# Eighteen block pairs in the MLP, with the copies, additions and gate parts around them placed anew

## The chip, the cores and the metric

One core of a Trainium2 chip runs the kernel. The metric is the device time of one execution in microseconds; several executions are taken, and their median is compared. The core has five engines that run side by side, each in the order of its own instruction list: PE (matmuls), DVE, ACT, POOL and SP. SP only issues transfers here; ACT and POOL can issue some too. Engines wait for each other through semaphores.

## The reference, cut to what matters

One layer of a decoder over 512 positions with model width 1024: a token-mixing half (sparse attention and a gated short convolution, merged by gates and projected by `w_o`), a layer norm, and then the half that the change is about:

```python
h = layer_norm(DEEPNORM_ALPHA * h + merged @ w_o[i], ln1_g[i], ln1_b[i])
gu = causal_dwconv(h @ w_ffn_up[i], ffn_conv_w[i], ffn_conv_b[i])
g_ffn, u_ffn = jnp.split(gu, 2, axis=-1)
ffn = (jax.nn.silu(g_ffn) * u_ffn) @ w_ffn_down[i]
ple = jax.nn.sigmoid(h @ w_ple_gate[i] + b_ple_gate[i]) * (p[i] @ w_ple[i])
h = layer_norm(DEEPNORM_ALPHA * h + ffn + ple, ln2_g[i], ln2_b[i])
```

`w_ffn_up` is 1024 x 5632 (2816 gate columns and 2816 up columns), `w_ffn_down` 2816 x 1024. All is float32.

## The kernel before, in words

**Precision.** Each matrix is split into a high part and a remainder, both in the matmul's 32-bit format, and a product is three matmuls: high by high, high by low, low by high. For weights `Chunk` does this: SP loads a raw tile `wr` of 128 x 1024 (L54; four buffers), ACT casts it to `wh` (L74), and DVE or POOL subtracts to get `wl` (L141). There are four buffers of `wh` and `wl`; a chunk is split up to three steps ahead of its use, if a buffer is free.

**Steps.** The program is a list of steps, and each engine gets its instructions in this order. For step i: first the splits (and loads) that are due (`advance`), then the functions registered for the step in `preps`, then the step's own matmuls and what follows them. Steps 0 to 5 are index queries, 6 (`at_first`) to 43 attention queries, convolution, attention, gates and branches. Steps 44 (`at_wo`) to 47 are the first column half of `w_o` for all four blocks of 128 positions, 24 matmuls a step; behind step 47 DVE adds the residual and takes statistics (L924, L186). Steps 48 to 51 are the second half, one block of positions a step. Behind the matmuls of each, DVE adds and normalises that block (`ln1`, L947, L931, L932), and PE transposes the block before it (`ln1_T`, tile xT). Step 52 is `ple1`. Steps 53 (`at_ple`) to 64 are the gate `h @ w_ple_gate`, and from 65 (`at_ff`) the up-projection's 22 pairs of a gate column tile and an up column tile follow, then the down-projection.

**Products with one block fewer.** Where two column tiles and two halves of the positions make a 2 x 2 block product, seven products of sums replace eight (`by_blocks`). A plain pair j takes two steps of 24 matmuls with 512 columns each. A pair in `BY_BLOCKS` (2 to 18) takes three steps of 24 and one of 12 matmuls with 256 columns, and needs two chunks that are sums of blocks of the weights. These sums are made in DRAM ahead of time: SP copies blocks into `ws` (`weight_copy`, two transfers of 256 KB each), and POOL issues transfers that add to them (`weight_add`, four of 256 KB a pair). The gate (sums by `gate_sums` on DVE of tiles `pgr` that `gate_load` brings, four times 512 KB) and the down-projection (`sum_copy`, `sum_add`, 24 each, 512 KB, tiles `sd`) do the same. The pairs' sums are made in two groups, `pairs[0]` (the first `EARLY`) and `pairs[1]`.

**Order of transfers.** `at_step(at, f, eng)` puts a transfer into step `at`; with an engine it is tied to that engine's progress: the engine writes a token, POOL reads it (tile behind, L1319) and then issues. Before, the early copies stood in steps 6 to 20, the early additions in 21 to 40, the copies of the late pairs in 30 to 40, their additions every fourth step from 63, all 24 copies of `sd` from 55 to 72, and the first 12 additions of `sd` every sixth step from 69. `gate_load` stood in steps 42 and 43, `gate_sums` in 45 and 46. The three tiles `pw` were loaded back in step 52 (L966). The gate's end (`gate_mult`, L1039; `gate_add`, L1043; four parts) stood in steps 68 to 74.

Of the kernel before, what the change touches and what calls it, by code (L numbers as in the profile page):

```python
# [11 lines left out]
OP = mybir.AluOpType  # L12
# [71 lines left out]
class Kern:  # L84
# [409 lines left out]
    def plan(self):  # L494
        nc, a = self.nc, self.a
# [321 lines left out]
        early = [(wa(8 + i, lo="vp"[i], resident=True), kind) for i, kind in enumerate("cx")]  # L817
# [27 lines left out]
        at_first = len(self.steps)  # L845
# [116 lines left out]
        def ple1(pc, w):  # L962
            def f():
                self.pw = [[self.k4(f"pw{h}{i}", F32, (P, 2, 512)) for i in range(2)] for h in range(2)]
                for i in range(3):
                    nc.sync.dma_start(self.pw[i // 2][i % 2], self.pwdram[i].rearrange("p (b n) -> p b n", b=2))  # L966
                act = [[t.rearrange("p (k t) -> p k t", k=2)[:, k] for t in (pc.hi, pc.lo)] for k in range(2)]
                for b in range(2, NB):
                    tb = slice(b * P, (b + 1) * P)
                    o = self.ps("ple")  # L970
                    for k in range(2):
                        wh, wl = (t.rearrange("p (k n) -> p k n", k=2)[:, k] for t in (w.hi, w.lo))
                        self.mm3(o, act[k][0][:, tb], act[k][1][:, tb], wh, wl, k == 0, k == 1)
                    nc.scalar.copy(self.pw[1][b // 2][:, b % 2], o)
            return f
# [6 lines left out]
        def gate_load(u):  # L982
            def f():
                gate_raw[u] = [self.k4(f"pgr{u}{i}") for i in range(4)]
                for i, t in enumerate(gate_raw[u]):
                    nc.sync.dma_start(t, a["w_b"][10 + 2 * i + u])
            return f

        def gate_sums(u):

            def f():
                ra, rb, rc, rd = gate_raw[u]
                for to, x, y in ((rd, rc, rd), (rc, ra, rc), (ra, ra, rd), (rb, rb, ra)):
                    nc.vector.tensor_tensor(to, x, y, op=OP.add)
            return f

        for u in range(2):
            self.preps.setdefault(at_wo - 2 + u, []).append(gate_load(u))
            self.preps.setdefault(at_wo + 1 + u, []).append(gate_sums(u))
        self.hblock, self.hsum = {}, {}  # L1000
        first_gate = [wb(10 + u, resident="halves", lo="p", lead=9) for u in range(2)]
        pc, w = chunk(a["p_T"]), wb(9)
# [1 line left out]

        at_ple = len(self.steps)
        self.gsum, self.gacc = {}, {}
        GATE = {"a": ("X", 0, 0), "b": ("Y", 1, 0), "cd": ("Z", None, 0), "acd": ("X", None, 2),
                "abcd": ("Z", 1, 1), "ac": ("X", None, 1), "d": ("X", None, 3)}

# [31 lines left out]
        def gate_add(f, t, i):  # L1041
            h = self.h1[2 * t + i][:, f * 512:f * 512 + 512]
            nc.vector.scalar_tensor_tensor(h, h, ALPHA, self.gsum[f, t][:, i], op0=OP.mult, op1=OP.add)  # L1043
# [115 lines left out]

        BY_BLOCKS = list(range(2, 19))
        EARLY = 13
        wsum = {j: [self.dram.tile([P, 1024], F32, name=f"ws{i}{j}", tag=f"ws{i}{j}") for i in range(2)]
                for j in BY_BLOCKS}

# [95 lines left out]
        def sum_copy(n, i):  # L1262
            return lambda: nc.sync.dma_start(sd[n][i], wd[base[n], i])

        def sum_add(n, i):
            return lambda: nc.gpsimd.dma_start(sd[n][i], adds[n](i), accum_op=OP.add, max_dma_last_dim=4096)

        at_ff = len(self.steps)
        self.row_sums = row_sums
# [2 lines left out]
            self.preps.setdefault(at_ple + at, []).append(f)  # L1272

        parts_of = [(0, 0), (0, 1), (1, 1), (1, 0)]
        for f, at in ((gate_bias, (6, 10, 13, None)), (gate_sigmoid, (7, 11, 14, 15)), (gate_mult, (15, 16, 18, 20)),
                      (lambda f, t: gate_add(f, t, 0), (15, 17, 19, 21)), (lambda f, t: gate_add(f, t, 1), (16, 17, 19, 21))):
            for x, n in zip(parts_of, at):
                if n is not None:
                    self.preps.setdefault(at_ple + n, []).append(lambda f=f, x=x: f(*x))
# [42 lines left out]

        pairs = BY_BLOCKS[:EARLY], BY_BLOCKS[EARLY:]
        for n, (j, i) in enumerate((j, i) for i in range(2) for j in pairs[0]):
            at_step(at_first + 15 * n // (2 * EARLY), weight_copy(j, i))
        for n, (j, i) in enumerate((j, i) for i in (0, 1, 3, 2) for j in pairs[0]):
            at_step(at_first + 15 + 21 * n // 56, weight_add(j, i), nc.vector)
        for n, (j, i) in enumerate((j, i) for j in pairs[1] for i in range(2)):  # L1330
            at_step(at_first + 24 + n * 3 // 2, weight_copy(j, i))
        for n, (j, i) in enumerate((j, i) for j in pairs[1] for i in (0, 1, 3, 2)):
            at_step(at_ff - 2 + 4 * n, weight_add(j, i), nc.scalar)
        for n, (name, i) in enumerate(copies):
            at_step(at_ple + 2 + n * 3 // 4, sum_copy(name, i))
            at = (4 + 6 * n if n < 12 else n_ff - 6 + (n - 12) * 5 // 4 if n < 17 else n_ff + 1 + 3 * (n - 17))
            at_step(at_ff + at, sum_add(name, i), nc.scalar)


        TAILC = 4  # L1340
# [289 lines left out]
```

## Time and profile before

| | |
|---|---|
| Median of 3 runs | 749.59 us (749.45 to 753.15) |
| Profiled execution | 751.02 us, span 749.3 us |
| Granted clock of PE, mean | 0.994 of full speed |
| PE busy | 736.3 us (98%) |
| DVE, ACT, POOL busy | 606.6, 403.6, 233.5 us |
| DMA | 172.48 MB, 230 GB/s mean |

The span runs from the first to the last instruction; the execution's time is a little longer. Matmuls overlap, so a busy PE isn't one at its peak; the distance between the starts of matmuls is the better measure. Tiles are named without their numbers: `pgr` is any of the gate's raw tiles. "x4" is the number of instructions that a row merges, and in brackets stands how long the engine was idle before them and what ended that. SPq is SP's list of issues.

### The profile page before, as it was taken

The numbers are of one execution on the slowest core, as the hardware profiler recorded it, in microseconds if no ns is written. First come the engines' busy times: TensorE is split into PE (matmuls) and PEld (weight loads), VectorE is DVE, ScalarE is ACT, GpSimd is POOL, SyncE is SP. The second block draws the span as 40 slices with busy tenths as digits, with TensorE's granted clock in tenths as the row PEclk, the third lists the DMA queues.
The fourth block names the chain that finished last, engine by engine and source line by source line (L and its number), as shares of the span: only waits on it lengthen the run. The fifth ranks groups of instructions, "written<-read, shape, count | busy, mean of one in ns | idle before, by whom it ended". The sixth has DMA issues, their size and how long they took to land.

```text
span 749.3 us, 11574 instructions
## 1 busy us (share of the span) xinstructions
PE 736.3 (98%) x4159; PEld 640.4 (85%) x4159; DVE 606.6 (81%) x1031; ACT 403.6 (54%) x671; POOL 233.5 (31%) x294
## 2 busy tenths in 40 slices
PE   9999999999999999998999999999999999999995
PEld 5998888888888888887888899999999988888885
DVE  5877999865666366769997899999998888978797
ACT  4557334457566325233465567676676653655540
POOL 4314656542412545435300122333311112121002
PEclk9999999999999999999999999999999999999998
DMA  9372597679756989993576999888997877999661
GB/s 350 103 279 99 169 382 233 203 222 212 165 102 159 254 222 305 319 370 113 204 302 206 345 266 270 239 256 215 239 266 217 232 219 171 265 266 281 223 212 56
DMA packets 57257, 172.48 MB, mean 230 GB/s; under 512 B 6720, under 2 KB 6848, under 8 KB 56816
## 3 DMA queue, kind: packets, MB, share of 16 engines
q1 hardware_dynamic: 41664, 135.29, 50.8%
q0 software_dynamic: 14384, 34.22, 25.3%
q10 hardware_dynamic: 1152, 2.25, 0.8%
q8 instruction: 32, 0.52, 0.3%
q14 instruction: 25, 0.20, 0.1%
HBM read 165.95 MB, written 66.58 MB: 310 GB/s over the span
## 4 chain that ended last, share of the span: by engine, by line
PE 49%; DVE 2%; DMA 1%; issue 0%; POOL 0%; ACT 0%; DVEq 0%; ACTq 0%
PE ffb L1212 20%; PE dn L1385 5%; PE dn L1384 5%; PE dn L1386 5%; PE ff L155 2%; PE ff L156 2%; PE ff L157 2%; PE pg L1026 2%; PE pg L1024 2%; PE pg L1025 2%; DMA wr<-in_w_a 1%; PE xT L122 1%; PE wo L799 1%; PE wo L800 1%; PE wo L801 1%; DVE ff L708 0%
## 5 line engine op out<-in xcount | busy, mean ns | idle before, releaser
L74 ACT CAST wh<-wr 128x1024 fp32r<-128x1024 f32 (+1 forms) x179 | 176.3, 990 | 98.8 <-PE dn L1386 21.0
L141 DVE TENSOR_TENSOR wl<-wr,wh 128x1024 fp32r<-128x1024 f32 (+1 forms) x162 | 191.1, 1195 | 34.7 <-ACT wh L74 33.7
L1319 POOL TENSOR_TENSOR behind<-token,neghalf 128x1 f32<-128x1 f32 x92 | 51.4, 588 | 306.9 <-ACT token L1318 208.5
L1212 PE MATMUL ffb<-hsl,wh 128*128 128x256 f32 x272 | 77.0, 283 | 0.0
L1212 PE MATMUL ffb<-hsh,wh 128*128 128x256 f32 x272 | 77.0, 283 | 0.0
L1212 PE MATMUL ffb<-hsh,wl 128*128 128x256 f32 x272 | 77.0, 283 | 0.0
L1212 PE MATMUL ffb<-h1T,wh 128*128 128x256 f32 x408 | 75.2, 284 | 0.8 <-ACT c L1235 0.8
L1212 PEld LDWEIGHTS ffb<-h1T,wh 128*128 128x128 f32 x408 | 63.6, 192 | 1.5 <-ACT c L1235 1.4
L141 POOL TENSOR_TENSOR wl<-wr,wh 128x1024 fp32r<-128x1024 f32 (+1 forms) x21 | 49.2, 2353 | 35.9 <-ACT wh L74 35.9
L1212 PE MATMUL ffb<-h1T,wl 128*128 128x256 f32 x204 | 57.7, 283 | 0.0
L1212 PEld LDWEIGHTS ffb<-hsh,wh 128*128 128x128 f32 x272 | 52.2, 192 | 0.0
L1212 PEld LDWEIGHTS ffb<-hsl,wh 128*128 128x128 f32 x272 | 52.2, 192 | 0.0
L1212 PEld LDWEIGHTS ffb<-hsh,wl 128*128 128x128 f32 x272 | 52.2, 192 | 0.0
L155 PE MATMUL gt<-hT,wh 128*128 128x512 f32 x128 | 50.6, 395 | 0.1
L157 PE MATMUL gt<-hT,wl 128*128 128x512 f32 x128 | 49.9, 390 | 0.0
L156 PE MATMUL gt<-hT,wh 128*128 128x512 f32 x128 | 49.8, 389 | 0.0
L1212 PEld LDWEIGHTS ffb<-h1T,wl 128*128 128x128 f32 x204 | 39.1, 192 | 0.0
L173 POOL TENSOR_TENSOR rstd<-veps,neghalf 128x1 f32<-128x1 f32 x12 | 11.7, 979 | 81.6 <-DVE veps L171 42.8
L1185 POOL DMA_DIRECT2D ws<-in_w_a x34 | 32.0, 1189 | 3.4 <-issue 3.0
L1185 POOL DMA_DIRECT2D ws<-ws x34 | 31.1, 1072 | 2.3 <-DVE sig L785 0.9
L155 PE MATMUL cv<-hT,wh 128*128 128x512 f32 x80 | 31.4, 392 | 0.0
L155 PE MATMUL ff<-h1T,wh 128*128 128x512 f32 x80 | 31.1, 389 | 0.0
(337 smaller groups left out, 2021.0 us busy)
## 6 DMA issues: line engine op xcount, KB each, us to landing
wr<-in_w_a SPq DMA_DIRECT2D x63, 512.0 KB, 4.9
ws<-in_w_a SPq DMA_DIRECT2D x68, 256.0 KB, 6.4
wr<-ws SPq DMA_DIRECT2D x34, 512.0 KB, 6.2
ws<-in_w_a POOLq DMA_DIRECT2D x34, 256.0 KB, 8.2
ws<-ws POOLq DMA_DIRECT2D x34, 256.0 KB, 7.7
wr<-in_w_b SPq DMA_DIRECT2D x15, 512.0 KB, 11.4
wr<-in_w_dn SPq DMA_DIRECT2D x15, 512.0 KB, 5.6
wr<-in_w_a SPq DMA_DIRECT2D x17, 256.0 KB, 6.4
```

What stands on the lines that cost most here:

```text
L74: nc.scalar.copy(hi, raw)
L141: (self.nc.vector if eng == "v" else self.nc.gpsimd).tensor_tensor(lo, raw, hi.bitcast(F32), op=OP.subtract)
L155: t.matmul(out, wh, xh, start=start, stop=False)
L156: t.matmul(out, wh, xl, start=False, stop=False)
L157: t.matmul(out, wl, xh, start=False, stop=stop)
L1024: nc.tensor.matmul(o, xh, wh, start=first, stop=False, skip_group_check=True)
L1185: return lambda: nc.gpsimd.dma_start(to, what, accum_op=OP.add, max_dma_last_dim=4096)
L1212: nc.tensor.matmul(o, l[:, c], r, start=start and c + i == 0, stop=stop and c == 3 and i == 2, skip_group_check=True)
L1319: nc.gpsimd.tensor_tensor(self.sm("behind", [P, 1], bufs=2), t, self.neghalf, op=OP.mult)
L1384: nc.tensor.matmul(o, ah, wh[:, i, c], start=first, stop=False, skip_group_check=bank == "X")
L1385: nc.tensor.matmul(o, ah, wl[:, i, c], start=False, stop=False, skip_group_check=bank == "X")
L1386: nc.tensor.matmul(o, al, wh[:, i, c], start=False, stop=last, skip_group_check=bank == "X")
```

## The change

- `BY_BLOCKS` begins at pair 1 instead of 2, so there are 18 block pairs, and `EARLY` is 14 instead of 13; four late pairs remain.
- 28 early weight copies and, between them, the 12 `sd` copies `cd` and `abcd` are put into steps 3 to 19. The early additions (56 instead of 52) follow in steps 21 to 41.
- The copies of the late pairs move to steps 48 to 51. The other 12 `sd` copies stand in steps 54 to 65, one each.
- From step 63 on, additions follow about every 1.83 steps: one of a late pair and one half (512 columns) of `ac` or `acd` in turn; these 12 additions become 24 of 256 KB.
- `gate_load(0)` moves from step 42 to 41 (`gate_load(1)` stays in 43), `gate_sums` from 45 and 46 to 44 and 45.
- The loads of `pw` move from step 52 to 54, 55 and 56, one each.
- The gate's last parts spread: multiplications in steps 66, 70, 74 and 79 instead of 68, 69, 71 and 73, additions up to step 83 instead of 74. A block pair begins at step 69, so the parts fall into block pairs 1 to 4 and the steps before.

```diff
--- before.py
+++ after.py
@@ -962,8 +962,6 @@
         def ple1(pc, w):
             def f():
                 self.pw = [[self.k4(f"pw{h}{i}", F32, (P, 2, 512)) for i in range(2)] for h in range(2)]
-                for i in range(3):
-                    nc.sync.dma_start(self.pw[i // 2][i % 2], self.pwdram[i].rearrange("p (b n) -> p b n", b=2))
                 act = [[t.rearrange("p (k t) -> p k t", k=2)[:, k] for t in (pc.hi, pc.lo)] for k in range(2)]
                 for b in range(2, NB):
                     tb = slice(b * P, (b + 1) * P)
@@ -995,8 +993,8 @@
             return f
 
         for u in range(2):
-            self.preps.setdefault(at_wo - 2 + u, []).append(gate_load(u))
-            self.preps.setdefault(at_wo + 1 + u, []).append(gate_sums(u))
+            self.preps.setdefault(at_wo - 3 + 2 * u, []).append(gate_load(u))
+            self.preps.setdefault(at_wo + u, []).append(gate_sums(u))
         self.hblock, self.hsum = {}, {}
         first_gate = [wb(10 + u, resident="halves", lo="p", lead=9) for u in range(2)]
         pc, w = chunk(a["p_T"]), wb(9)
@@ -1004,6 +1002,12 @@
 
         at_ple = len(self.steps)
         self.gsum, self.gacc = {}, {}
+
+        def ple_back(i):
+            return lambda: nc.sync.dma_start(self.pw[i // 2][i % 2], self.pwdram[i].rearrange("p (b n) -> p b n", b=2))
+
+        for i in range(3):
+            self.preps.setdefault(at_ple + 1 + i, []).append(ple_back(i))
         GATE = {"a": ("X", 0, 0), "b": ("Y", 1, 0), "cd": ("Z", None, 0), "acd": ("X", None, 2),
                 "abcd": ("Z", 1, 1), "ac": ("X", None, 1), "d": ("X", None, 3)}
 
@@ -1159,8 +1163,8 @@
 
 
 
-        BY_BLOCKS = list(range(2, 19))
-        EARLY = 13
+        BY_BLOCKS = list(range(1, 19))
+        EARLY = 14
         wsum = {j: [self.dram.tile([P, 1024], F32, name=f"ws{i}{j}", tag=f"ws{i}{j}") for i in range(2)]
                 for j in BY_BLOCKS}
 
@@ -1262,8 +1266,9 @@
         def sum_copy(n, i):
             return lambda: nc.sync.dma_start(sd[n][i], wd[base[n], i])
 
-        def sum_add(n, i):
-            return lambda: nc.gpsimd.dma_start(sd[n][i], adds[n](i), accum_op=OP.add, max_dma_last_dim=4096)
+        def sum_add(n, i, cols=slice(0, 1024)):
+            return lambda: nc.gpsimd.dma_start(sd[n][i][:, cols], adds[n](i)[:, cols], accum_op=OP.add,
+                                               max_dma_last_dim=4096)
 
         at_ff = len(self.steps)
         self.row_sums = row_sums
@@ -1272,8 +1277,8 @@
             self.preps.setdefault(at_ple + at, []).append(f)
 
         parts_of = [(0, 0), (0, 1), (1, 1), (1, 0)]
-        for f, at in ((gate_bias, (6, 10, 13, None)), (gate_sigmoid, (7, 11, 14, 15)), (gate_mult, (15, 16, 18, 20)),
-                      (lambda f, t: gate_add(f, t, 0), (15, 17, 19, 21)), (lambda f, t: gate_add(f, t, 1), (16, 17, 19, 21))):
+        for f, at in ((gate_bias, (6, 10, 13, None)), (gate_sigmoid, (7, 11, 14, 15)), (gate_mult, (13, 17, 21, 26)),
+                      (lambda f, t: gate_add(f, t, 0), (14, 18, 23, 28)), (lambda f, t: gate_add(f, t, 1), (15, 20, 25, 30))):
             for x, n in zip(parts_of, at):
                 if n is not None:
                     self.preps.setdefault(at_ple + n, []).append(lambda f=f, x=x: f(*x))
@@ -1322,19 +1327,28 @@
 
 
 
+
         pairs = BY_BLOCKS[:EARLY], BY_BLOCKS[EARLY:]
-        for n, (j, i) in enumerate((j, i) for i in range(2) for j in pairs[0]):
-            at_step(at_first + 15 * n // (2 * EARLY), weight_copy(j, i))
+        early = [weight_copy(j, i) for i in range(2) for j in pairs[0]]
+        first, late = copies[:12], copies[12:]
+        for i, (name, k) in enumerate(late):
+            early.insert(3 * i + 2, sum_copy(name, k))
+        for n, f in enumerate(early):
+            at_step(3 + 17 * n // len(early), f)
         for n, (j, i) in enumerate((j, i) for i in (0, 1, 3, 2) for j in pairs[0]):
             at_step(at_first + 15 + 21 * n // 56, weight_add(j, i), nc.vector)
         for n, (j, i) in enumerate((j, i) for j in pairs[1] for i in range(2)):
-            at_step(at_first + 24 + n * 3 // 2, weight_copy(j, i))
-        for n, (j, i) in enumerate((j, i) for j in pairs[1] for i in (0, 1, 3, 2)):
-            at_step(at_ff - 2 + 4 * n, weight_add(j, i), nc.scalar)
-        for n, (name, i) in enumerate(copies):
-            at_step(at_ple + 2 + n * 3 // 4, sum_copy(name, i))
-            at = (4 + 6 * n if n < 12 else n_ff - 6 + (n - 12) * 5 // 4 if n < 17 else n_ff + 1 + 3 * (n - 17))
-            at_step(at_ff + at, sum_add(name, i), nc.scalar)
+            at_step(at_wo + 4 + n // 2, weight_copy(j, i))
+        for n, (name, i) in enumerate(first):
+            at_step(at_ple + 1 + n, sum_copy(name, i))
+        those = [weight_add(j, i) for j in pairs[1] for i in (0, 1, 3, 2)]
+        rows_of = [sum_add(name, i, slice(512 * h, 512 * h + 512)) for name, i in first for h in range(2)]
+        n = len(those)
+        turns = [x for two in zip(those, rows_of) for x in two] + rows_of[n:]
+        for n, f in enumerate(turns):
+            at_step(at_ff - 2 + 11 * n // 6, f, nc.scalar)
+        for n, (name, i) in enumerate(late):
+            at_step(at_ff + (n_ff - 6 + n * 5 // 4 if n < 5 else n_ff + 1 + 3 * (n - 5)), sum_add(name, i), nc.scalar)
 
 
         TAILC = 4
```

## Rows read from the trace of the kernel before

**Rows 1.** Busy time of the engines, page of before (busy us, share, instructions).
```profile
PE 736.3 (98%) x4159; PEld 640.4 (85%) x4159; DVE 606.6 (81%) x1031; ACT 403.6 (54%) x671; POOL 233.5 (31%) x294
```

**Rows 2.** Waits of PE (us in total, times, longest).
```profile
PE xT L122 <- DVE hr L932: 2.5, 1, 2.5
...
PE ffb L1212 <- ACT c L1235: 0.8, 2, 0.4
```

**Rows 3.** Timeline of PE, starts of MLP steps (start, us, line, out<-in).
```profile
425.25 0.39 PE L155 MATMUL ff<-h1T,wh 128*128 128x512 f32 x1
...
430.69 0.40 PE L1212 MATMUL ffb<-h1T,wh 128*128 128x256 f32 x2
...
439.32 0.40 PE L1212 MATMUL ffb<-h1T,wh 128*128 128x256 f32 x2
...
449.40 0.40 PE L1212 MATMUL ffb<-h1T,wh 128*128 128x256 f32 x2
```

**Rows 4.** Timeline of PE around the transposes of the first norm.
```profile
349.25 0.39 PE L801 MATMUL wo<-wh,mT 128*128 128x512 f32 x1
...
352.10 1.97 PE L122 MATMUL xT<-ident,hr 128*128 128x128 f32 x8 [2.46 <-DVE hr L932]
...
355.44 0.40 PE L800 MATMUL wo<-wl,mT 128*128 128x512 f32 x1
...
359.76 0.39 PE L801 MATMUL wo<-wh,mT 128*128 128x512 f32 x1
...
361.79 0.39 PE L800 MATMUL wo<-wl,mT 128*128 128x512 f32 x1
```

**Rows 5.** Timeline of DVE, 325 to 355 us.
```profile
325.14 5.01 DVE L994 TENSOR_TENSOR pgr<-pgr,pgr 128x1024 f32<-128x1024 f32 x4 [0.31 <-DMA pgr<-in_w_b]
...
330.07 1.22 DVE L141 TENSOR_TENSOR wl<-wr,wh 128x1024 fp32r<-128x1024 f32 x1
...
333.93 8.06 DVE L994 TENSOR_TENSOR pgr<-pgr,pgr 128x1024 f32<-128x1024 f32 x4 [2.64 <-DMA pgr<-in_w_b]
...
347.19 0.67 DVE L947 TENSOR_TENSOR hr<-wo,hr 128x512 f32<-128x512 f32 x1
...
350.74 1.31 DVE L932 SCALAR_TENSOR_TENSOR hr<-hr,rstd,b 128x1024 f32<-128x1024 f32 x1 [0.47 <-POOL rstd L173]
...
351.97 2.35 DVE L141 TENSOR_TENSOR wl<-wr,wh 128x1024 fp32r<-128x1024 f32 x2
```

**Rows 6.** Windows: stretch, us; busy PE, PEld, DVE, ACT, POOL; granted clock, DMA share, GB/s.
```profile
94.73:136.44 41.71, 41.71 (x194) 34.34 (x192) 40.02 (x89) 16.84 (x24) 26.67 (x16) 1.00 0.77 273
...
280.00:333.00 53.00, 53.00 (x236) 43.88 (x235) 36.37 (x42) 19.04 (x23) 24.53 (x30) 1.00 1.06 341
...
340.00:360.00 20.00, 17.54 (x76) 14.39 (x75) 18.74 (x27) 4.42 (x6) 9.23 (x8) 0.91 0.28 103
```

**Rows 7.** Timeline of SP: first and last of eight ws copies, 280 to 304 us.
```profile
280.89 0.50 SPq L1173 DMA_DIRECT2D ws<-in_w_a  x1
...
303.31 0.60 SPq L1177 DMA_DIRECT2D ws<-in_w_a  x1
```

**Rows 8.** DMA queues of SP and POOL, page of before (packets, MB, share).
```profile
q1 hardware_dynamic: 41664, 135.29, 50.8%
...
q0 software_dynamic: 14384, 34.22, 25.3%
```

**Rows 9.** Windows of block pairs (columns as in rows 6).
```profile
430.69:602.17 171.48, 170.67 (x1417) 170.05 (x1416) 156.82 (x233) 117.83 (x217) 46.19 (x60) 1.00 0.88 244
...
449.40:459.48 10.08, 10.08 (x86) 10.08 (x85) 8.83 (x14) 6.87 (x13) 2.10 (x3) 1.00 0.84 267
...
520.92:531.00 10.08, 10.08 (x87) 10.08 (x86) 9.92 (x15) 7.19 (x13) 4.31 (x6) 1.00 1.08 260
```

**Rows 10.** Timelines of POOL and ACT in one block pair.
```profile
506.16 1.52 POOL L1266 DMA_DIRECT2D sdac<-in_w_dn  x1
...
516.47 1.05 ACT L74 CAST wh<-wr 128x1024 fp32r<-128x1024 f32 x1 [2.56 <-DMA wr<-in_w_a]
```

## The prediction

> **What bounds the kernel.** I read the busy table first: PE is busy 98% of the span [rows 1], so a change pays by taking matmuls away or by closing a gap of PE. The waits of PE come next. Past the first microseconds only two matter [rows 2]: one of 2.5 us at the transposes xT, and two of 0.4 us in the block pairs. Every other transfer, DVE operation and copy is hidden behind matmuls, and matters only if it makes a new wait. Costs are summed against the profiled execution (span 749.30 us, its run 751.02) and the sum is taken off the median, 749.59.
>
> **The extra block pair.** A plain step of 24 matmuls with 512 columns starts at 425.25 and ends where the block pairs start, at 430.69: 5.44 us, 10.88 a pair. A whole block pair (three steps of 24 and one of 12 matmuls with 256 columns) takes from 439.32 to 449.40, 10.08 us [rows 3]. Pair 1 changes from the one to the other: **-0.80 us**.
> The Trainium skill (TensorE: Matmul & The Clock Gate, Back-to-back issue gap) puts a warm matmul at N/2.4 + 2.5 ns; by it the pair would save 48 x 215.8 - 84 x 109.2 ns = 1.19 us, and the sum below would be lower by 0.4. The rows (227 and 120 ns a matmul) disagree with it and are used.
>
> **The wait at xT, and the sums moved ahead of it.** The last wo matmul before it starts at 349.25, the fifth after the transposes at 355.44; at the next block of tokens the same distance is 359.76 to 361.79. So the place costs 6.19 - 2.03 = 4.16 us: 2.46 of waiting and 1.7 of slow matmuls behind it [rows 4]; the granted clock of 340 to 360 us is 0.91, that of 280 to 333 is 1.00 [rows 6], so for part of it PE ran at the lower of its two levels. What is late is DVE's normalisation of block 0 (L932, ends 352.05). Followed back on DVE [rows 5]: the chain from the second half's addition (347.19) to there is 4.86 us; four additions and statistics stand before it, from 341.99; and before those the second gate sums (L994), which began at 333.93 after DVE had waited 2.64 us for their loads and took 8.06 us, while the first took 5.01.
> The diff runs both sums a step (5.44 us) earlier. That helps only if the loads come earlier too. The first load moves up a step, the second stays at its step. In 280 to 333 us the DMA engines are saturated, share 1.06 [rows 6], so the second load lands when the work ahead of it is done. Out of that stretch go eight SP copies of 256 KB, from 280.89 to 303.31 [rows 7]. Into it, just behind, come the last four of 56 instead of 52 POOL additions. From the queues' totals [rows 8] SP moves 135.29 MB in 50.8% of 749.3 us, 0.74 us per 256 KB; POOL's queue 34.22 MB in 25.3%, 1.45 us. That is 5.9 us out and 5.8 in: the second load still lands near 333.9.
> The sums now stand ahead of the split of the sixth wo chunk (L141 at 330.07 in [rows 5]): it belongs to the step after, whose splits the diff leaves where they are. So DVE would stand idle longer in front of the sums, with that split queued behind them, end the sums at 342.0 and the split at 343.2. PE wants it in the first step of the second half, which begins two steps before the transposes (349.48 - 10.88 = 338.6), with the eighth matmul, at 340.2. It would wait 3.0 us there and pay the same 1.7 of slow matmuls: 4.7 late, at the transposes by 354.2. DVE's additions (5.2) and chain (4.86) behind the split end at 353.7, so the transposes no longer wait; the kernel before stood there, slow matmuls included, at 349.48 + 4.16 = 353.6. At the next block DVE comes 2.35 for two splits ([rows 5], 351.97) and 4.86 later, 360.9, PE after transposes and a step (0.8 + 5.44) at 360.4: another 0.5. Taken: 0.6 + 0.5, about **+1.0 us**. Ends: loads in by 331 give xT back and keep a wait of 0.7 at the next block (DVE at 349.3 + 7.2, PE at 349.5 + 6.3), -3.5; loads 2 us later than before, +3.0.
>
> **Additions behind products, in halves.** The 17 block pairs before took 171.48 us [rows 9]; their 1416 matmuls up to there at 10.08/84 make 169.92, so 1.56 us are lost in them, 0.8 of it the waits of ffb [rows 2]. One of these places: ACT stood until 516.47 for a weight load, 2.56 us, a 512 KB addition having been issued by POOL at 506.16 right behind one of 256 KB [rows 10], and the PSUM copy (L1235) that PE waited for stood behind it on ACT. Now 256 KB follow every other step, and this meeting is gone, but the bytes aren't. Between 0 and -1.56 I take **-1.2**, as the pair of [rows 9] that ends on time shows what single additions cost: nothing.
>
> **DVE in the first block pairs.** Three parts of the gate now fall into block pairs 1 to 4, each a multiplication (1.22 us, as L141) and two additions (0.67, as L947 in [rows 5]): 7.7 us against 5.1 before, in pair 2. A pair leaves DVE 10.08 - 8.83 = 1.25 us, or 0.16 where POOL is busy 4.31 us [rows 9]. Bounds: 0, as the 5.1 us before made no wait, and 2.7, all that four pairs of 1.25 don't take. Nearer to the first: **+0.4**.
>
> **What I cost at nothing.** Forty copies instead of 26 in the early steps: in 94.73 to 136.44 the DMA share is 0.77 [rows 6]; seven steps with 0.6 more copies, of 1.48 us each, add 6.4 us in 41.7, so 0.92, and no wait of PE for a weight is in [rows 2]. Were these engines full, the chunks behind would be late by those 6.4 us. The loads of pw and the copies at the gate: SP no longer stands before pw's slots with the copies behind it; nobody on PE waited for either. The POOL instructions of 12 additional half additions and their tokens on ACT are short and are counted in the slower rival.
>
> **Sum.** -0.8 + 1.0 - 1.2 + 0.4 = -0.6 us: span 748.7, median **749.0 us**.
>
> **Rivals.** *The loads come early* (chance 0.32). If additions cost less than their queue's mean while SP's loads run beside them, or SP's copies more, the second load lands by 331, the sums end before the sixth split is wanted, and the xT wait goes: -0.8 - 3.5 - 1.2 + 0.4 = -5.1, 744.5 us. For it: the copies' removal is the earlier of the two; against it: share 1.06 leaves no idle time to gain. *Half of that* (0.15): landing at 332 to 333, 746 to 748 us. *Slower: DVE becomes the bound of the block pairs* (0.07). In the pair with POOL at 4.31 us DVE is busy 9.92 of 10.08 [rows 9]; with more additions per pair POOL is as busy in all of them. It decides when DVE's work in a pair passes 10.08; at 0.25 us over it in 18 pairs the time is 749.0 + 4.5 = 753.5 us. Against it: in the row with 9.92 PE had no gap.
> The Trainium skill (SBUF — State Buffer, Who interferes with whom) says that GpSimd and a DVE operation with two SBUF inputs lock one shared port against each other; the trace agrees as far as 8.06 against 5.01 us goes.
>
> **Chances.** My forecast with its own spread, 747.8 to 751, has 0.43; 0.03 is left for a late early weight. A median of this kernel can tell about 0.5%, 3.75 us: faster than 745.84 is the first rival and a little of the second (0.34), slower than 753.34 the last, and the upper end of late loads (0.09), the rest is no change. The range reaches from the first rival and 0.9 below it (the rest of the gain bounded under additions and DVE) to the late loads, 743.6 to 751.2.
>
> **What would show it.** The pair: block matmuls rise by 84, plain ones fall by 48. The sums: where L994 begins the second time (333.9 forecast; by 331 the rival), and whether PE waits on wo for a split (L141) near 340 or on xT near 349. The additions: no pair over 10.2 us. DVE: waits of ffb in the first four block pairs. I am wrong by most if the second gate load lands several us earlier or later than 333.9, or if a PE wait appears before 280 us.

## The result and the profile after

The changed kernel takes **756.25 us** (median of 7 runs, 753.7 to 757.53) against 750.22 us for the kernel before in the same comparison (7 runs, 749.05 to 753.15): a ratio of 1.0064, 95% interval 1.0043 to 1.0085. It is slower by 0.64%, 5 us above the upper end of the predicted range. The profiled execution has a span of 754.7 us, 5.4 more than before.

Where the time went is read by laying the two timelines of PE side by side and subtracting, stage by stage, the start of the same matmul (after minus before, in us):

| Start of, in the trace before | after minus before |
|---|---|
| attention queries, 72.97 | -0.48 |
| first convolution step behind them, 94.73 | +0.39 |
| gate matmuls gt, 163.09 | +2.57 |
| first half of wo, 316.84 | +2.55 |
| second transposes xT, 359.99 | +7.28 |
| first up-projection step, 403.49 | +7.35 |
| first plain step behind the block pairs, 602.17 | +5.33 |
| down-projection, 636.30 | +5.32 |

The first 0.48 us come from the first microseconds of the span. Then there are three places: 3.05 us lost between 73 and 163 us, 4.8 lost in wo, 2.0 gained in the block pairs. Lines of the page of after that answer to [rows 1, 8]: PE's busy time, the queues of SP and of POOL.

```profile
PE 737.5 (98%) x4195; PEld 642.0 (85%) x4195; DVE 610.3 (81%) x1040; ACT 405.9 (54%) x689; POOL 256.3 (34%) x326
...
q1 hardware_dynamic: 42528, 137.12, 52.0%
q0 software_dynamic: 16688, 35.27, 26.5%
```

The waits of PE after (us in total, times, longest) name the second place at once, and of the first only the last links:

```profile
PE wo L800 <- DVE wl L141: 5.5, 1, 5.5
...
PE lg L164 <- ACT sig L769: 0.8, 1, 0.8
PE qa L157 <- POOL wl L141: 0.5, 1, 0.5
```

**The early stage.** PE's waits there are 0.8 us and less, so the chain has to be followed back through the engines that feed it. It ends at a load that no row of the prediction holds: `w_uk` (128 x 512, raw weights for the attention keys), issued on ACT's own queue and cast by ACT. Timeline of ACT in the kernel before, then after:

```profile
63.61 0.34 ACTq L600 DMA_DIRECT2D wuk_raw<-in_w_uk  x1
...
66.75 0.62 ACT L602 CAST wuk<-wuk_raw 128x512 fp32r<-128x512 f32 x1 [1.67 <-DMA wuk_raw<-in_w_uk]
```

```profile
64.28 0.33 ACTq L600 DMA_DIRECT2D wuk_raw<-in_w_uk  x1
71.27 0.62 ACT L602 CAST wuk<-wuk_raw 128x512 fp32r<-128x512 f32 x1 [6.66 <-DMA wuk_raw<-in_w_uk]
```

It landed 3.1 us after its issue before, 7.0 after. The timeline of SP after shows what is new in front of it: eight copies issued from 56.29 to 63.82 (the first, the fifth and the eighth are shown).

```profile
56.29 0.60 SPq L1177 DMA_DIRECT2D ws<-in_w_a  x1
...
58.85 0.60 SPq L1267 DMA_DIRECT2D sdcd<-in_w_dn  x1
...
63.82 0.59 SPq L1177 DMA_DIRECT2D ws<-in_w_a  x1
```

In the six profiles that leave this load behind the moved copies it landed 5.6 to 7.0 us after its issue, with six to eight copies in front; in the three without them (before, experiments 11 and 12) it took 3.1 to 3.5.

The Trainium skill (DMA: Bandwidth & Descriptors, Issuing engines are not separate DMA queues) says that transfers begun by different engines run on the same 16 DMA engines and interleave; the trace agrees: a queue of its own did not keep this load from taking 3.9 us more.

ACT works in order, so everything behind the cast was late: the next ReLU of the index scores, and with it DVE. DVE before, then after:

```profile
71.72 6.56 DVE L568 SCALAR_TENSOR_TENSOR score<-rl,widx,score 128x512 f32<-128x512 f32 x6 [2.65 <-ACT rl L566]
```

```profile
74.34 6.56 DVE L568 SCALAR_TENSOR_TENSOR score<-rl,widx,score 128x512 f32<-128x512 f32 x6 [5.76 <-ACT rl L566]
```

From there DVE picks keys without a gap until 145 us, before and after, so its 2.63 us stayed, and PE, which needs the picked keys, was 2.57 late at 163.09.

**wo.** DVE after, 327 to 361 us ([rows 5] are the same instructions before):

```profile
327.17 5.01 DVE L992 TENSOR_TENSOR pgr<-pgr,pgr 128x1024 f32<-128x1024 f32 x4 [3.05 <-DMA pgr<-in_w_b]
332.09 1.22 DVE L141 TENSOR_TENSOR wl<-wr,wh 128x1024 fp32r<-128x1024 f32 x1
338.05 8.04 DVE L992 TENSOR_TENSOR pgr<-pgr,pgr 128x1024 f32<-128x1024 f32 x4 [4.74 <-DMA pgr<-in_w_b]
346.01 2.28 DVE L141 TENSOR_TENSOR wl<-wr,wh 128x1024 fp32r<-128x1024 f32 x1
```

The split now stands behind the second sums, as forecast. The sums began at 338.05, which is 335.5 on the axis of before (2.55 less) and 1.6 later than 333.93; and the split took 2.28 us instead of 1.22. PE waited for it and then ran slowly (timeline of PE; the row at [rows 4] for the wait before is now 0.2 us):

```profile
342.51 0.39 PE L799 MATMUL wo<-wh,mT 128*128 128x512 f32 x1
348.35 0.79 PE L800 MATMUL wo<-wl,mT 128*128 128x512 f32 x1 [5.45 <-DVE wl L141]
348.94 0.63 PE L801 MATMUL wo<-wh,mT 128*128 128x512 f32 x1
...
354.06 0.49 PE L801 MATMUL wo<-wh,mT 128*128 128x512 f32 x1
354.39 0.40 PE L799 MATMUL wo<-wh,mT 128*128 128x512 f32 x1
```

**Windows after** (columns as in [rows 6]): the slow matmuls, the stretch of the gate loads, the early copies, and the block pairs (these answer to [rows 6, 9]).

```profile
348.35:354.06 5.71, 5.71 (x13) 4.46 (x14) 5.09 (x8) 1.31 (x2) 2.33 (x2) 0.50 0.64 221
...
280.00:333.00 53.00, 53.00 (x236) 43.90 (x235) 37.39 (x52) 18.87 (x23) 28.29 (x42) 1.00 1.02 292
427.16:607.50 180.34, 180.34 (x1502) 180.10 (x1501) 167.82 (x249) 126.82 (x242) 64.27 (x84) 1.00 0.88 232
95.12:136.83 41.71, 41.71 (x193) 34.35 (x192) 39.96 (x92) 15.24 (x23) 26.65 (x15) 1.00 0.93 345
```

At a granted clock of 0.50 (1.2 GHz) the fourteen matmuls from 348.35 to 354.39 took 6.04 us instead of 14 x 0.227 = 3.18: 2.9 us are lost to the clock. The early copies raised the DMA share from 0.77 to 0.93, as forecast, and PE lost nothing between 95 and 137 us; the loss began ahead of that window and showed in full behind it. The gate stretch stayed full (1.02), but moved 292 GB/s instead of 341: more of it were additions. POOL's queue moved 6.29 MB in it instead of 4.79, and its last weight addition was issued at 312.82 instead of 305.91, among the gate's loads. The 1500 matmuls of the block pairs took 180.34 us; at 10.08/84 they make 180.00, so 0.34 us are lost in them instead of 1.56, and no wait of ffb is left.

### The profile page after: what moved, and what is told of

Read it like the earlier page. It is cut to its first block, busy times and chain, and to the rows that moved or that the text cites. A ratio compares the mean times of both kernels' runs of the same rounds, so it can differ in the third digit from the quotient of the medians.

```text
span 754.7 us, 11708 instructions
## 1 busy us (share of the span) xinstructions
PE 737.5 (98%) x4195; PEld 642.0 (85%) x4195; DVE 610.3 (81%) x1040; ACT 405.9 (54%) x689; POOL 256.3 (34%) x326
## 3 DMA queue, kind: packets, MB, share of 16 engines
q0 software_dynamic: 16688, 35.27, 26.5%
## 4 chain that ended last, share of the span: by engine, by line
PE 69%; DMA 14%; DVE 5%; issue 4%; POOL 4%; ACT 3%; SPq 1%; DVEq 0%; ACTq 0%; POOLq 0%
PE ffb L1216 24%; PE dn L1399 5%; PE dn L1398 5%; PE dn L1400 5%; DMA ws<-in_w_a 3%; PE gt L155 3%; POOL wl L141 2%; PE gt L156 2%; PE gt L157 2%; DMA pgr<-in_w_b 2%; PE ff L155 2%; PE ff L156 2%; PE ff L157 2%; DMA wr<-in_w_b 2%; PE pg L1030 2%
## 5 line engine op out<-in xcount | busy, mean ns | idle before, releaser
L1324 POOL TENSOR_TENSOR behind<-token,neghalf 128x1 f32<-128x1 f32 x108 | 68.9, 666 | 301.7 <-ACT token L1323 219.7
L1216 PE MATMUL ffb<-hsl,wh 128*128 128x256 f32 x288 | 81.5, 283 | 0.0
L1216 PE MATMUL ffb<-hsh,wl 128*128 128x256 f32 x288 | 81.5, 283 | 0.0
L1216 PE MATMUL ffb<-hsh,wh 128*128 128x256 f32 x288 | 81.5, 283 | 0.0
L1216 PE MATMUL ffb<-h1T,wh 128*128 128x256 f32 x432 | 79.4, 283 | 0.0
L1216 PEld LDWEIGHTS ffb<-h1T,wh 128*128 128x128 f32 x432 | 67.4, 192 | 0.1
L1216 PE MATMUL ffb<-h1T,wl 128*128 128x256 f32 x216 | 61.3, 284 | 0.0
L1216 PEld LDWEIGHTS ffb<-hsh,wh 128*128 128x128 f32 x288 | 55.3, 192 | 0.0
L1216 PEld LDWEIGHTS ffb<-hsl,wh 128*128 128x128 f32 x288 | 55.3, 192 | 0.0
L800 PE MATMUL wo<-wl,mT 128*128 128x512 f32 x64 | 26.3, 411 | 5.5 <-DVE wl L141 5.5
```

The costliest lines, as they stand in the source:

```text
L800: nc.tensor.matmul(o, act[:, 0, tb], wl, start=False, stop=False)
L1216: nc.tensor.matmul(o, l[:, c], r, start=start and c + i == 0, stop=stop and c == 3 and i == 2, skip_group_check=True)
L1324: nc.gpsimd.tensor_tensor(self.sm("behind", [P, 1], bufs=2), t, self.neghalf, op=OP.mult)
```

## The experiments

Engines in the expectations: TensorE is PE, VectorE DVE, ScalarE ACT, GpSimd POOL. Each kernel ran beside the kernel before on one chip; the ratio is to that. The kernel before took 750.22 us in the comparison of the changed kernel, 751.71 in that of experiments 1 to 4, 751.33 in 5 to 8 and 751.29 in 9 to 12, so kernels of different comparisons are better compared by their ratios than by their medians. The middle columns are profile readings as in the table above: how much later than in the trace before PE began the gate matmuls (163.09), the up-projection (403.49) and the first step behind the block pairs (602.17).

| Kernel | median us | ratio, 95% interval | 163.09 | 403.49 | 602.17 |
|---|---|---|---|---|---|
| changed kernel | 756.25 | 1.0064 (1.0043 to 1.0085) | +2.57 | +7.35 | +5.33 |
| load of w_uk first | 755.86 | 1.0041 (1.0026 to 1.0056) | +0.70 | +4.97 | +4.31 |
| sums back | 753.99 | 1.0020 (0.9999 to 1.0042) | +1.24 | +3.02 | +2.49 |
| early copies alone | 755.96 | 1.0053 (1.0035 to 1.0071) | +0.62 | +6.66 | +6.45 |
| additions sooner | 753.45 | 1.0014 (0.9993 to 1.0034) | +2.43 | +3.62 | +2.93 |
| three repairs | 750.21 | 0.9989 (0.9976 to 1.0002) | +1.13 | -1.21 | -1.23 |
| loads and additions sooner | 756.33 | 1.0075 (1.0051 to 1.0099) | +0.85 | +6.55 | +5.15 |
| only the gate loads sooner | 749.93 | 0.9976 (0.9955 to 0.9997) | +2.23 | -0.08 | -0.87 |
| no extra pair | 752.08 | 1.0007 (0.9994 to 1.0021) | +0.61 | +3.04 | +1.48 |
| all repairs, turns apart | 746.87 | 0.9933 (0.9907 to 0.9958) | +1.38 | -1.85 | -4.18 |
| the same without the pair | 747.36 | 0.9945 (0.9926 to 0.9964) | +1.34 | -1.88 | -3.45 |
| before, gate loads sooner | 755.52 | 1.0053 (1.0029 to 1.0078) | -0.42 | +4.06 | +4.53 |
| before, halves alone | 748.82 | 0.9957 (0.9937 to 0.9977) | -0.12 | -1.07 | -2.64 |

**1. The load of w_uk first.**

```diff
+        def uk_load():
+            self.wuk_raw = self.k2("wuk_raw")
+            nc.scalar.dma_start(self.wuk_raw, a["w_uk"])
...
+        self.preps.setdefault(2, []).append(uk_load)
         self.preps.setdefault(5, []).append(uk_prep)
```

> The changed kernel with one edit: the load of w_uk (128x512, ScalarE's queue) is issued three steps sooner, ahead of the first early copy; its cast stays where it is. Theory A (one load behind the copies): in the changed kernel this load landed 7.0 us after its issue instead of 3.1, ScalarE waited 6.7 us for it and held up the score sums and the pick of keys on VectorE by 2.6 us, and TensorE lost 3.0 us between 73 and 166 us. It expects ScalarE's wait gone, VectorE's score step at 71 to 72 us instead of 74.3, and 753.2 us (3 less than 756.2). Rival B (forty copies slow the matmuls and weights in general): the load moves but TensorE still comes 2 to 3 us late to 166 us, and the time stays at 755.5 to 756.5.

ACT's wait for the load is gone, DVE's score step began at 72.48 and PE's delay at 163.09 fell from 2.57 to 0.70: theory A holds for the stage. The load itself was no faster in its new place, 6.3 us from issue to landing, but ACT wants it only 18.8 us after its issue. The 0.7 that is left is the repair's own: POOL's subtraction for `w_uk` now runs at 65.40, beside DVE's scores, and twelve of these take 10.83 us instead of 9.80. But the time did not fall by 3 us: the ratio went from 1.0064 to 1.0041, some 1.7 us (the medians, from different comparisons, differ by 0.4), and the intervals of the two overlap. The profile shows 1.4 us given back in the seventh block pair, 11.69 us long (timelines of POOL and ACT):

```profile
475.71 0.81 POOL L1273 DMA_DIRECT2D sdac<-in_w_dn  x1
...
477.03 0.81 POOL L1192 DMA_DIRECT2D ws<-ws  x1 [0.30 <-issue]
```

```profile
485.36 0.62 ACT L74 CAST wh<-wr 128x512 fp32r<-128x512 f32 x1 [1.43 <-DMA wr<-in_w_a]
487.50 1.05 ACT L74 CAST wh<-wr 128x1024 fp32r<-128x1024 f32 x1 [1.52 <-DMA wr<-ws]
...
488.54 0.36 ACT L1236 COPY c<-ffb 128x256 f32<-128x256 f32 x1
```

Two additions went out 1.3 us apart, two weight chunks issued beside them landed 9.0 us after their issue, and the PSUM copy (L1236) that PE waits for stood behind their casts. In the changed kernel's profile these two additions stood 2.6 us apart (478.11 and 480.73), and the seventh pair took 10.08 us.

**2. The sums back**, one step later, as before the change.

```diff
-            self.preps.setdefault(at_wo + u, []).append(gate_sums(u))
+            self.preps.setdefault(at_wo + 1 + u, []).append(gate_sums(u))
```

> The changed kernel with the gate sums one step later, where they were before; the gate loads stay where the change put them. Theory C (the split of a wo chunk stands behind the sums on VectorE): the 5.5 us wait of TensorE in the second half of wo is gone, a wait at xT of about 4 us comes back (2.5 before, plus 1.6 because the second gate load lands that much later), and the time falls by about 3.2 us to 753.0. Rival D (the sums are late because their load is late, so their place does not matter): the wait only changes its name, and the time stays within 0.7 us of 756.2.

As theory C expects: no wait in wo, and the old one is back, longer (waits of PE): 

```profile
PE xT L122 <- DVE hr L932: 4.2, 1, 4.2
```

From 316.84 to 403.49 PE lost 1.8 us (1.21 to 3.02) instead of 4.8.

**3. The early copies alone**, in the kernel before: its early copies are replaced by these lines, and the twelve copies that they move ahead go out of steps 55 to 72 (not shown).

```diff
+        early = [weight_copy(j, i) for i in range(2) for j in pairs[0]]
+        first, late = copies[:12], copies[12:]
+        for i, (name, k) in enumerate(late):
+            early.insert(3 * i + 2, sum_copy(name, k))
+        for n, f in enumerate(early):
+            at_step(3 + 17 * n // len(early), f)
...
```

> The kernel before with one part of the change: the block-sum copies for the early pairs and twelve of the copies for the down projection start at step 3, beside the index queries. Theory A: the load of w_uk lands 3 to 4 us later, TensorE comes to 166 us about 3.0 us late, and the kernel takes 752.6 to 753.2 us against 749.6 to 750.2 of before. Rival B2 (the loss comes with the extra pair's four copies or with other parts): within 0.7 us of before.

Slower by 0.53%, so this part alone can cost what the whole change cost. But theory A's 3.0 us at 166 are not there: the load landed 5.6 us after its issue and PE was 0.62 late. The profiled execution (757.46, above the median) lost 6.1 us in wo: DVE's first gate sums waited 4.67 us and began at 330.10, and PE waited at xT:

```profile
PE xT L122 <- DVE hr L932: 7.3, 1, 7.3
```

The transfers issued from 280 us on are those of before, in the same order and 1 to 3 us later; in 300 to 310 and 310 to 320 the DMA engines were as full and moved 282 and 299 GB/s, against 314 and 337 in the trace before. Why they moved less is not settled by one profile.

**4. The weight additions two steps sooner.**

```diff
-            at_step(at_first + 15 + 21 * n // 56, weight_add(j, i), nc.vector)
+            at_step(at_first + 13 + 21 * n // 56, weight_add(j, i), nc.vector)
```

> The changed kernel with the 56 weight additions two steps sooner. Theory E (the additions still in the DMA engines when the gate loads are issued make these late): the second gate load lands 3 us or more sooner than at 338.0 us, TensorE's wait in the second half of wo shrinks from 5.5 us to 1 to 2.5, and the time falls by 3 to 4.5 us to 751.7 to 753.2. Rival F (the loads are late for their place in the queue, behind the weight chunks of wo): they land at 337 to 338 us as before this edit, and the time stays within 0.7 us of 756.2.

Theory E holds: the second gate load landed at 332.4 instead of 338.0, the wait in wo fell to 3.2 us, the time by 2.8 us between the medians and by 0.5% (3.7 us) between the ratios. That it did not fall further is DVE's: it began the sums at 332.51, but they took 11.21 us, because POOL split chunks all the while.

**5. Three repairs**: the edits of 1 and 4 (three steps instead of two) and

```diff
-            self.preps.setdefault(at_wo + u, []).append(gate_sums(u))
+            self.preps.setdefault(at_wo + 2 * u, []).append(gate_sums(u))
```

> The changed kernel with three repairs: the load of w_uk ahead of the early copies, the weight additions three steps sooner, and the second gate sums one step later, behind the split of the wo chunk. Theory (A, C and E together): TensorE comes to 166 us under 1 us late, the second gate load lands by 331 us, there is no wait in the second half of wo and one of 2 to 3 us at xT; the time is 750 to 751.5 us, 5 us less than the changed kernel and no more than before. Rival: the repairs share one cause and add little to each other; 753 us, as the best single one.

The time is as expected, 750.21 us: the repairs add up. The second load landed at 324.9, and at xT 1.4 us in two waits are left. The seventh pair took 12.34 us and ate the gain of the block pairs.

**6. Loads and additions sooner**: the edit of 1, additions four steps sooner, and

```diff
-            self.preps.setdefault(at_wo - 3 + 2 * u, []).append(gate_load(u))
+            self.preps.setdefault(at_wo - 5 + 2 * u, []).append(gate_load(u))
```

> The changed kernel with the load of w_uk first, the weight additions four steps sooner and both gate loads two steps sooner; the sums stay where the change put them. Theory H (all of the loss in wo, and the wait at xT of the kernel before too, is the landing of the gate loads): the second load lands by 326 us, the sums end by 337 us, neither the wait in wo nor that at xT is left, and the time is 746 to 748.5 us, below both kernels. Rival I (the eight tiles of the gate are not free sooner, or the sums then meet the splits on VectorE and GpSimd): the loads land at 330 us or later and the time stays at 750.5 to 752.

A miss for both, H's time by 8 us. The loads landed by 325.9 as theory H has it, but the additions, now beside the last early copies, made a new wait near 180 us: the load of `w_uv` landed 18.2 us after its issue, ACT stood for it, and PE came 9.75 us late to 184 (waits of ACT):

```profile
ACT wh L74 <- DMA wr<-in_w_uv: 8.0, 1, 8.0
```

Three steps sooner (5.) made no such wait.

**7. Only the gate loads sooner**: the diff of 6, nothing else.

> The changed kernel with both gate loads two steps sooner and nothing else. If the place of the loads in the queue decides (theory H), the second lands 5 us or more sooner, TensorE's wait in wo falls from 5.5 us below 1, and the time falls by 4.5 us to 751.5. If the additions and the DMA engines' backlog decide (theory E), the loads are issued sooner and land at most 3 us sooner, the wait stays at 3 us or more, and the time is 753.5 to 755.

Theory H's side, and 1.6 us better than it says: 749.93 us. The second load landed at 332.1, 5.9 us sooner, and the wait in wo is gone, and with it the slow matmuls: the granted clock stayed at 1.00 there. Besides, the chunks of wo now load behind the gate's tiles, so POOL had none to split yet, and DVE's second sums took 5.00 us instead of 8.04. DVE, then POOL:

```profile
332.24 5.00 DVE L992 TENSOR_TENSOR pgr<-pgr,pgr 128x1024 f32<-128x1024 f32 x4 [1.81 <-DMA pgr<-in_w_b]
337.16 1.22 DVE L141 TENSOR_TENSOR wl<-wr,wh 128x1024 fp32r<-128x1024 f32 x1
```

```profile
338.37 4.78 POOL L141 TENSOR_TENSOR wl<-wr,wh 128x1024 fp32r<-128x1024 f32 x2 [13.97 <-ACT wh L74]
```

In 4., where they met, DVE and POOL show:

```profile
332.51 11.21 DVE L992 TENSOR_TENSOR pgr<-pgr,pgr 128x1024 f32<-128x1024 f32 x4 [2.52 <-DMA pgr<-in_w_b]
```

```profile
332.42 5.74 POOL L141 TENSOR_TENSOR wl<-wr,wh 128x1024 fp32r<-128x1024 f32 x2 [8.46 <-ACT wh L74]
```

The Trainium skill (SBUF — State Buffer, Who interferes with whom) has a DVE instruction with both inputs in SBUF contend with what POOL reads; the trace agrees, 1.25 us an addition alone and up to 2.8 beside POOL's splits.

**8. No extra pair.**

```diff
-        BY_BLOCKS = list(range(1, 19))
-        EARLY = 14
+        BY_BLOCKS = list(range(2, 19))
+        EARLY = 13
```

> The changed kernel with seventeen block pairs (pair 1 plain again); all else as changed. By the predicted term alone (0.80 us for the pair) the time rises to 757.0. Theory J (the pair's four additions, which come last and just ahead of the gate loads, cost more than the pair saves): the second gate load lands 2 to 4 us sooner, TensorE's wait in wo falls from 5.5 to 2 to 3.5 us, and the time falls to 753.5 to 755.

Theory J: 752.08 us, 4.2 below the changed kernel. The second load landed at 331.5, the wait in wo is 3.2 us. The pair's saving of 0.8 was bought with some 5 us elsewhere. Part of it, 2 us at 163.09, goes with how late w_uk landed: 5.9 us after its issue here, with six copies issued in front of it, 7.0 in the changed kernel, with eight. It need not be the pair's doing: in experiments 2 and 4, with the pair, seven and eight copies stood there and PE was 1.24 and 2.43 late.

**9. All repairs, turns apart**: the edits of 1, 4 and 6's loads (not its additions), and the late additions every second step.

```diff
-            at_step(at_ff - 2 + 11 * n // 6, f, nc.scalar)
+            at_step(at_ff - 2 + 2 * n, f, nc.scalar)
```

> The changed kernel with the load of w_uk first, both gate loads two steps sooner, the weight additions two steps sooner, and the late additions one every second step instead of eleven in six turns. Theory K (two of the late additions issued 1.3 us apart make two weight chunks of the seventh block pair land 9 us after their issue, and TensorE loses 1.5 us there): every block pair takes 10.08 to 10.2 us, the delay against before falls by 2.3 us from the gate to the last pair, and with no wait in wo the time is 746 to 747.5 us. Rival L (the seventh pair's loss has another cause, such as ScalarE's order): a pair of 11.5 us or more is left and the time is 748.5 to 750.

As theory K expects: **746.87 us**, 0.67% faster than before (0.42 to 0.93%) and faster than both kernels. All waits of PE behind the first 50 us:

```profile
PE lg L164 <- ACT sig L772: 0.8, 1, 0.8
...
PE xT L122 <- DVE hr L935: 0.5, 1, 0.5
...
PE lg L164 <- DVE pT L145: 0.2, 1, 0.2
```

No block pair took more than 10.12 us (windows, the 18 pairs):

```profile
417.96:597.99 180.03, 180.03 (x1501) 180.03 (x1500) 166.65 (x250) 127.73 (x242) 52.44 (x82) 1.00 0.89 230
```

With six turns in eleven steps, five of the seven kernels with 18 pairs had a seventh pair of 11.57 to 12.34 us; with every second step there was none. That additions issued close together make the long pair, as theory K has it, is not shown: the kernel without the pair (8.) had two 0.7 us apart and no long pair, and in 5. those ahead of the longest one stood 2.4 us apart, nearly as in the changed kernel:

```profile
469.53 0.81 POOL L1273 DMA_DIRECT2D sdac<-in_w_dn  x1
...
471.93 0.80 POOL L1192 DMA_DIRECT2D ws<-ws  x1
```

**10. The same with seventeen pairs** (the diff of 8 on 9).

> The same kernel as the one with all repairs, but with seventeen block pairs (pair 1 plain). With nothing waiting for its four copies and four additions, the pair should be worth the predicted 0.80 us: the time is 0.5 to 1.1 us above the repaired kernel with eighteen. If the pair's transfers still cost something wherever they lie, the two are the same or the one without is faster.

The pair is worth 0.73 us in the profiles (-4.18 against -3.45) and 0.49 in the medians (nine of the eleven executions with it lie below the fastest without it), close to the predicted 0.80, once nothing waits for its transfers.

**11. The kernel before with the gate loads sooner.**

```diff
-            self.preps.setdefault(at_wo - 2 + u, []).append(gate_load(u))
+            self.preps.setdefault(at_wo - 5 + 2 * u, []).append(gate_load(u))
```

> The kernel before with both gate loads sooner (five and three steps ahead of wo instead of two and one) and nothing else. If the kernel before also paid for late gate loads (its wait at xT of 2.5 us and the 1.7 us of slow matmuls), the wait goes and it takes 747 to 748.5 us. If its twelve late copies and additions hold the DMA engines all the same, the loads land within 2 us of before and the time stays within 0.7 us of before.

Neither: 0.53% slower. The first gate load landed at 318.1, 7 us sooner than before, the second at 331.9, 2 us sooner; but the chunks of wo stood behind them, DVE waited for a chunk's cast, began the second sums at 335.54 and, beside POOL's splits, took 10.14 us. PE's wait at xT rose from 2.5 to 6.5 us. What is moved ahead here only makes something else late. The same edit helped the changed kernel (7.), which has taken the eight copies of the late pairs out of this stretch; that this is the reason is likely and not tested alone.

**12. The kernel before with the halves alone**: the first twelve additions of `sd` in halves, in turn with the weight additions.

```diff
...
+        turns = [x for two in zip(those, rows_of) for x in two] + rows_of[n:]
+        for n, f in enumerate(turns):
+            at_step(at_ff - 2 + 11 * n // 6, f, nc.scalar)
...
```

> The kernel before with one part of the change: the first twelve of the additions for the down projection in halves, taking turns with the weight additions. By the predicted term its three long block pairs (10.37, 10.75 and 10.69 us) become 10.08 to 10.2 and the time falls by 1.2 to 1.6 us to 750. Rival: the turns make a new long pair, as the seventh in some runs of the changed kernel, and the time stays within 0.5 us of before.

Faster by 0.43% (0.23 to 0.63). All 17 pairs took 10.07 to 10.08 us, and the block pairs gave 1.57 (-1.07 to -2.64), the whole of what was lost there [rows 9]. The other 1.07 came at wo, where nothing was edited and the second gate load landed as before (333.5 us, 333.8 before). There PE waited 2.33 us at xT and the granted clock did not fall, as it did in the trace before (0.91 in this window, [rows 6]):

```profile
340.00:360.00 20.00, 17.20 (x84) 13.89 (x82) 18.74 (x28) 4.90 (x7) 8.91 (x8) 1.00 0.27 100
```

So of the 2.5 us between the medians 1.57 are shown to be the edit's.

## Why the prediction was wrong

By the terms of the sum, predicted and read from the two profiles: pair, additions and DVE -1.6, measured -2.0; the wait at xT and the sums +1.0, measured +4.8; "What I cost at nothing" 0, measured +3.05. With the 0.48 us of the first microseconds these make the 5.4 us between the profiles, where -0.6 was forecast. The other 1.2 us of the miss, 756.25 against 749.0, are the base: the sum was worked out on an execution of 751.02 us and taken off a median of 749.59.

- **The step that failed** is "What I cost at nothing". It looked at the weight chunks of PE, on SP's queue, in 94.73 to 136.44, and there it was right: share 0.93, no chunk late. It did not go through what else is loaded where the copies begin, at 56 us. One load of 256 KB on ACT's queue stood there with 1.7 us of waiting already, ACT behind it in order, and behind ACT a DVE that has no gap until 145 us. In five of the six profiles with the load behind the copies the delay of DVE's score step (0.62, 0.63, 1.30, 2.28 and 2.63 us) is that of PE at 163.09 (0.62, 0.61, 1.24, 2.23 and 2.57); in experiment 4, with the additions sooner, it is 2.01 and 2.43. With the load first PE's delay fell to 0.70. The text named a PE wait ahead of 280 us as what would make it wrong.
- **The wait at xT, and the sums moved ahead of it**: the mechanism was right in each link (split behind the sums, PE waits in wo, the wait at xT goes), and experiments 2, 4 and 7 took it apart; the size was off, and this is the larger part of the miss. Of the 3.8 us between +1.0 and +4.8, 1.6 are the load's landing, 1.1 the split at 2.28 us beside POOL, and 1.2 the slow matmuls, 2.9 us where 1.7 had been taken. Against these stands the wait at the next block, 0.2 instead of 0.5 (it was mis-summed: 343.2 + 5.2 + 4.86 is 353.3 and not 353.7, which makes it 0.1). That leaves 0.2 that I can't place. For the landing, 5.9 us out and 5.8 in was no balance. The mean price of POOL's queue is nearly as taken, 26.5% of 754.7 us for 35.27 MB or 1.49 us per 256 KB; but what came in, came last, among the gate's loads, and the stretch moved 292 GB/s instead of 341. With the additions sooner or four fewer (experiments 4 and 8) the second load landed at 332.4 and 331.5 instead of 338.0. The end of +3.0 for a load 2 us later held the first of the three only.
- **The extra block pair**: right as a term (0.73 against 0.80), but only where its transfers lie in slack. As placed, taking it out made the kernel 4.2 us faster; its eight transfers were priced in the sums of other steps and not as the pair's.
- **Additions behind products, in halves**: right as a term, -1.2 of 1.56 in the changed kernel's profile and the whole 1.57 in the kernel before (experiment 12). But "no pair over 10.2 us" did not hold: the sixth pair took 10.31 in the changed kernel's profile, and in five of the six other kernels with 18 pairs and these turns the seventh took 11.57 to 12.34, which ate the gain.
- **DVE in the first block pairs**: nothing, not +0.4; pairs 1 to 4 took 10.07 to 10.08 us.
- **Rivals.** "The loads come early" did not happen: the second landed 1.6 us later on its own axis. Nor did DVE become the bound: no wait of ffb is left after.

What stays open: why the DMA engines, as full as before, moved 10 to 11% less in 300 to 320 us when only the early copies were moved (experiment 3); what makes the seventh pair long, and how often; and whether the extra pair has a part in how late w_uk's load comes (experiment 8).

## What to carry to other kernels

Before a copy is called hidden, list every load that is issued in the stretch it moves into, on every queue, and follow the engine that waits for it in its order: here a load of 256 KB that came 3.9 us late made PE 2.6 us late 90 us further on. Where the DMA engines are full, price a transfer by what lands behind it, not by its own time; and when work is added ahead of a split on an in-order engine, ask what the engine does when that work's data are late. A saving in matmuls (0.8 us here) is worth its number only after its transfers have found slack.

## What was not expected of the hardware

- The same four additions of DVE (128 x 1024, 32-bit) took 5.00 us alone and 8.0 to 11.2 us beside POOL's subtractions. With the second load landing at 332.1 and 332.4 us, the sums that ran alone left no wait in wo, and those beside POOL one of 3.2 us (experiments 7 and 4).
- What the lower clock (granted 0.50) cost behind a wait did not follow the wait's length: nothing after 2.33 us (experiment 12), 1.7 after 2.46 (before), 1.6 and 2.7 after 3.2 (experiments 4 and 8), 2.9 after 5.45 (the changed kernel) and 2.0 after 5.8 (experiment 1). Between the first and the last stage the clock did not fall at all in the profiles of experiments 5, 7, 9, 10 and 12, and once in each of the others, so some of what the repairs gain is clock.
- Single executions of one kernel spread by several us: the kernel before took 749.41 to 758.99 in one comparison, with a mean granted clock of 0.992 to 0.998; with all repairs eleven executions beside it lay within 746.68 to 748.64, with 0.996 to 0.998. What else makes the spread is not shown.
